# Norm, gate and weight-splitting arithmetic moved from GpSimd to VectorE in a two-block transformer kernel

## The chip, the cores and the metric

One core of one Trainium2 chip runs the whole program. The metric is device microseconds of one execution. The kernel before took 3540.33 us (median of 3 runs, 3538.97 to 3543.59). The engines are TensorE (matmul; PE in the profile, its weight loads PEld), VectorE (DVE), ScalarE (ACT), GpSimd (POOL) and SyncE (SP, which here only issues DMAs). Each engine works through its own queue in order.

## The reference, cut to what matters

The input x is 512 tokens of 1024 features, in float32. The first block repeats twice:

```
x = layer_norm(ALPHA * x + 0.5 * swiglu(x, ffn_w_in[i, 0], ffn_w_out[i, 0]), ln_g[i, 0], ln_b[i, 0])
mix = token_mix(x, ...)      # stick-breaking attention, gated delta rule, short convolution
x = layer_norm(ALPHA * x + mix, ln_g[i, 1], ln_b[i, 1])
x = layer_norm(ALPHA * x + 0.5 * swiglu(x, ffn_w_in[i, 1], ffn_w_out[i, 1]), ln_g[i, 2], ln_b[i, 2])
ple = jax.nn.sigmoid(x @ ple_w_gate[i] + ple_b_gate[i]) * (p[i] @ ple_w_proj[i])
x = layer_norm(ALPHA * x + ple, ln_g[i, 3], ln_b[i, 3])
```

The second block has one layer of dilated window attention and one of grouped attention, each with attention over 256 memory tokens, and an RMS norm ahead of the projections.

## The kernel before

Features lie on the partitions, as 8 tiles of 128 (`KD`), tokens on the free axis; `HALF` are the two halves of 256 tokens, `ALL` all 512. Nearly every float32 operand of a matmul is split in two parts of type float32r: the upper part is a copy in that type, the lower part is the value minus the upper part. A product is three matmuls: lower times upper, upper times lower, upper times upper.

**Weights** go through `Kern.weight` (L145 to L156): a DMA into `wst` (2 buffers), ScalarE's copy into `whi` (L153; 5 buffers), and a subtraction into `wlo` (L154; 5 buffers), by VectorE, or by the engine that the caller names. A `wst` buffer is free for the next load once the subtraction has read it. Where no engine is named and `K.fence` is set, the subtraction is put behind the instruction in `K.fence` on VectorE. `K.fence` is set once, by `row_rsqrt` in `RMS.scale_time` for the second half of the tokens at the end of the second `ple`: it is the last step of that norm's scale. The callers that name GpSimd: `ffn` for its first 4 tile pairs (in the first ffn of all only for one tile), all 34 units of `mixer` in each of the two layers, `ple` for its gate units (the last four of the second ple excepted), `mem_kv` of layer 0 inside the second ple (8 units) and `q_mem` of layer 0 (4 units).

**Layer norm** is the class `LN`. `add` (L267) runs after each output tile f: VectorE adds it to x (L271). At f = 0 the mean over that tile is taken through a matmul with `mean_r`, ScalarE copies it to `c` (`ln_c`, L282), and c is subtracted from all 8 tiles of x: from tile 0 by VectorE (L283), from the other seven by GpSimd (L285). For the other tiles ScalarE makes the square (L290), VectorE adds the tile to the running sum `ln_s` (L296), and the square is added to `ln_q`: by GpSimd for f = 1 to 5 (L299), by VectorE for f = 6 and 7 (L301, L303). `begin` sums `ln_s` and `ln_q` over partitions on TensorE (`ln_st`, L315), then runs a chain of small VectorE instructions on 128x2 (L319 to L323, the inverse root in L231 to L239), spreads mean and scale over the partitions on TensorE (`ln_M`, `ln_B`, L253) and subtracts the mean (L332). `end` multiplies by the scale (L343), lets ScalarE apply gain and bias (L345), copies pairs of tiles into `xh` (VectorE, L352) and makes `xl` (GpSimd, L353). `xh` and `xl` are what the next stage's matmuls read.

At the end of a stage the first half of the tokens is normed while TensorE still works on the second half, and the next stage starts on the first half while the second is normed.

**RMS norm** ahead of the second block: `RMS.write_time` splits 8 tiles for each half; every third subtraction from tile 1 on is GpSimd's (L1307).

The order on TensorE in `mixer` is written out by `weave`; elsewhere, and on the other engines, the tile framework's planner places the instructions by a timeline of its own when the program is built.

GpSimd also has work that stays: x restored from xh + xl at the end of the mixer (L592), two products in the mixer (L784, L940), rope (L1185, L1186), the softmax scale in layer A (L1379) and `RMS.add` (L1327).

Of the kernel before, what the change touches and what calls it, by code (L numbers as in the profile page):

```python
# [10 lines left out]
F = mybir.dt.float32  # L11
# [9 lines left out]
D = 1024  # L21
KD = D // 128
# [235 lines left out]
class LN:  # L258
# [7 lines left out]
    def add(self, f, ps, tk, scale):  # L266

        K, nc = self.K, self.K.nc
        y = self.y[:, f, tk]
        n = tk.stop - tk.start  # L270
        add = nc.vector.scalar_tensor_tensor(y, ps, scale, y, op0=OP.mult, op1=OP.add)  # L271
        if f == 0:
            if self.c is None:
                self.c = K.t2(name="ln_c")
                self.s = K.t2(name="ln_s")
                self.q = K.t2(name="ln_q")
            r = K.t2((128, n), FR, name="ln_r")
            nc.scalar.copy(r, y)
            p = K.mps((128, n), name="ln_p")
            nc.tensor.matmul(p, lhsT=K.mean_r, rhs=r, start=True, stop=True)  # L280
            c = self.c[:, tk]
            nc.scalar.copy(c, p)  # L282
            nc.vector.tensor_sub(y, y, c)  # L283
            for k in range(1, KD):
                nc.gpsimd.tensor_sub(self.y[:, k, tk], self.y[:, k, tk], c)  # L285
            nc.vector.tensor_copy(self.s[:, tk], y)
            nc.scalar.activation(self.q[:, tk], y, AF.Square)
            return
        sq = K.t2((128, n), name="ln_sq")
        square = nc.scalar.activation(sq, y, AF.Square)  # L290
        if f == KD - 1:
            self.lead = add, square
            if tk.start:
                self.last = sq
                return
        nc.vector.tensor_add(self.s[:, tk], self.s[:, tk], y)  # L296
        q = self.q[:, tk]
        if f < KD - 2:
            nc.gpsimd.tensor_add(q, q, sq)  # L299
        elif f == KD - 2:  # L300
            nc.vector.scalar_tensor_tensor(q, q, self.eps * D / 128, sq, op0=OP.add, op1=OP.add)  # L301
        else:
            nc.vector.tensor_add(q, q, sq)  # L303
# [31 lines left out]
    def end(self, tk, xh=None, xl=None, lead=True):  # L335

        K, nc = self.K, self.K.nc
        n = tk.stop - tk.start
        B = self.B.pop(tk.start)
        for k0 in range(0, KD, 2):  # L340
            ks = slice(k0, k0 + 2)
            y = self.y[:, ks, tk]
            mul = nc.vector.tensor_mul(y, y, B.unsqueeze(1).to_broadcast([128, 2, n]))  # L343
            for k in (k0, k0 + 1):
                act = nc.scalar.activation(self.y[:, k, tk], self.y[:, k, tk], AF.Identity, scale=self.g[:, k:k + 1],  # L345
                                           bias=self.b[:, k:k + 1])
                if lead and tk.start == 0 and k == 2:
                    K.behind([act], self.lead[1])
            if lead and tk.start == 0 and k0 == 2:
                K.behind([mul], self.lead[0])  # L350
            if xh is not None:
                nc.vector.tensor_copy(xh[:, ks, tk], y)  # L352
                nc.gpsimd.tensor_sub(xl[:, ks, tk], y, xh[:, ks, tk].bitcast(F))  # L353


def ffn(K, l, j, x, xh, xl, ln, aside=None, load=None):

    nc = K.nc
    w_in, w_out = K.i["ffn_w_in"], K.i["ffn_w_out"]
    hh, hl = [], []  # L360

    def unit(f, u):
        wh, wl = K.weight(w_in[l, j, 2 * f + u], D, nc.gpsimd if (f < 4 if load is None else f == 0 and u) else None)
        return wh.rearrange("p (k c) -> p k c", k=KD), wl.rearrange("p (k c) -> p k c", k=KD)

    def parts(W):
        return [(W[0][:, k], W[1][:, k]) for k in range(KD)]

    def moving(tk):
        return [(xh[:, k, tk], xl[:, k, tk]) for k in range(KD)]  # L370

    def swish(f, ps, tk):
        s = K.t2((128, tk.stop - tk.start), name="silu")
        K.looked.append(nc.scalar.activation(s, ps[0], AF.Silu))  # L374
        nc.vector.tensor_mul(s, s, ps[1])  # L375
        K.split(hh[f][:, tk], hl[f][:, tk], s)

    for f in range(NF):
        hh.append(K.t2(dt=FR, name="hh"))
        hl.append(K.t2(dt=FR, name="hl"))  # L380
    if load:

        first, W = 1, []
        for k in range(0, KD, 2):
            if k < 4:
                W.append(parts(unit(0, k // 2)))
            load(k)
        ps = [K.acc(name="pgu") for _ in range(2)]
        K.mm3_side([(ps[u], W[u], moving(ALL)) for u in range(2)])
        swish(0, ps, ALL)  # L390
    else:
        first = 2
        Ws = [[unit(f, 0), unit(f, 1)] for f in range(first)]
        for tk in HALF:
            ps = [[K.acc((128, 256), name="pgu") for _ in range(2)] for _ in range(first)]
            K.mm3_side([(ps[f][u], parts(Ws[f][u]), moving(tk)) for f in range(first) for u in range(2)])
            for f in range(first):
                swish(f, ps[f], tk)
        Ws = None
    for f in range(first, NF):  # L400
        W = [unit(f, 0), unit(f, 1)]
        ps = []
        for u in range(2):
            ps.append(K.acc(name="pgu"))
            K.mm3(ps[u], list(zip(parts(W[u]), moving(ALL))))
        swish(f, ps, ALL)
        if aside and f == NF // 2:
            K.masks()
            aside()

    def out_tile(f, W, tk):
        p = K.acc((128, tk.stop - tk.start), name="pfo")
        K.mm3(p, [((W[k // 8][0][:, k % 8], W[k // 8][1][:, k % 8]), (hh[k][:, tk], hl[k][:, tk])) for k in range(NF)])
        ln.add(f, p, tk, 0.5 / ALPHA)

    def out_units(f):
        W = []
        for k0 in range(0, NF, 8):
            n = min(8, NF - k0)
            a, b = K.weight(w_out[l, j, f, :, k0 * 128:(k0 + n) * 128], n * 128)  # L420
            W.append((a.rearrange("p (k c) -> p k c", k=n), b.rearrange("p (k c) -> p k c", k=n)))
        return W

    for f in range(KD - 1):
        out_tile(f, out_units(f), ALL)
    W = out_units(KD - 1)
    out_tile(KD - 1, W, HALF[0])
    ln.begin(HALF[0])
    out_tile(KD - 1, W, HALF[1])
    ln.end(HALF[0], xh, xl)  # L430
    ln.begin(HALF[1])
    ln.end(HALF[1], xh, xl)
# [40 lines left out]
def mixer(K, l, xh, xl, ln):  # L473

    nc, mm, tp = K.nc, K.mm, K.turn
# [15 lines left out]
    dt_b = cload([128, 4], ci["gdn_dt_bias"][l], "gdt")  # L491

    def unit(src):
        wh, wl = K.weight(src, D, nc.gpsimd)
        return wh.rearrange("p (k c) -> p k c", k=KD), wl.rearrange("p (k c) -> p k c", k=KD)

    def b3(col, n=128):
# [517 lines left out]
def ple(K, l, x, xh, xl, ln, rms=None, aside=None):  # L1015

    nc = K.nc
# [17 lines left out]
    for f in range(KD):  # L1035
        p = K.acc(name="ppp")
        K.mm3(p, [((Wp[f // 4][0][:, f % 4, k], Wp[f // 4][1][:, f % 4, k]), (ph[k], pl[k])) for k in range(2)])
        c = K.t2(name="pp")
# [1 line left out]
        pp.append(c)  # L1040

    def unit(f, spare=False):
        return K.unit(K.i["ple_w_gate"][l, f], None if spare else nc.gpsimd, spare)

    def some(fs, W, tk):

# [216 lines left out]
class RMS:  # L1263
# [36 lines left out]
    def write_time(self, tk):  # L1300
        K, nc = self.K, self.K.nc
        i = slice(tk.start // 4, tk.stop // 4)
        for k in range(KD):
            hv = self.h[k].rearrange("p (i c) -> p i c", c=4)
            xh, xl = by_time(self.xh[:, k])[:, i], by_time(self.xl[:, k])[:, i]
            nc.scalar.copy(xh, hv)
            (nc.gpsimd if k % 3 == 1 else nc.vector).tensor_sub(xl, hv, xh.bitcast(F))  # L1307

    def add(self, f, ps, tk):

# [203 lines left out]
def drive(first, second=(), rate=1.0):  # L1514

    live = [[0.0, n, iter(gen), 1.0 / r] for n, (gen, r) in enumerate(((first, 1.0), (second, rate)))]
    while live:
        s = min(live, key=lambda a: a[:2])
        try:
            next(s[2])  # L1520
            s[0] += s[3]
        except StopIteration:
            live.remove(s)
# [176 lines left out]
def program(tc, ins, outs):  # L1700
    with ExitStack() as ctx:
        K = Kern(ctx, tc, ins, outs)
        nc = K.nc
        xh = K.ph.tile([128, KD, S], FR, name="xh")
# [5 lines left out]
        with tc.tile_pool(name="px", bufs=1) as px:  # L1710
# [5 lines left out]
            with K.region(g=49):  # L1716
# [12 lines left out]
                parts = []  # L1729
# [4 lines left out]
                def memory(stage):  # L1734
                    if stage == 0:
                        R = K.t2((128, 256), name="mem_r")
                        nc.sync.dma_start(out=R, in_=memd[:, 2048:])
                        parts.extend(mem_parts(K, 0, R, [K.t2((128, 2, 256), FR, name="mem_p") for _ in range(8)]))
                    else:
                        drive(mem_kv(K, 0, *parts, mk, mv, nc.gpsimd, (stage - 1,)))  # L1740
                ple(K, DEPTH - 1, x, xh, xl, LN(K, x, *load_ln(K, DEPTH - 1, 3), eps), RMS(K, lambda f: x[:, f], xh, xl, g),
                    memory)
                for j in range(2):
# [178 lines left out]
```

## Time and profile before

| | |
|---|---|
| median of 3 runs | 3540.33 us (3538.97 to 3543.59) |
| the profiled execution | 3544.78 us |
| its span, first to last instruction | 3543.0 us |
| TensorE busy | 3410.4 us (96%) |
| VectorE busy | 1946.4 us (55%) |
| ScalarE busy | 1245.0 us (35%) |
| GpSimd busy | 723.7 us (20%) |
| mean granted TensorE clock | 0.975 of full speed |

Busy time is the time in which an engine had an instruction in work, whether it moved forward or stood. The granted clock is TensorE's: 1.0 is 2.4 GHz, 0.5 is 1.2 GHz; a figure between them over a stretch is the mean of the two. A wait's releaser is the instruction whose end let the waiting one start.

The stages in the trace, by time of start: ffn of layer 0 (15 us), mixer (about 380), second ffn (747), ple (1123), ffn of layer 1 (1216), mixer (1587), ffn (1955), ple with the memory projections (2331), and from about 2474 the second block's layers A and B.

### The profile page before, as it was taken

The page shows a single profiled execution, that of the slowest core. Times are in us where ns is not written, and L with a number is a line of the kernel's source. Part 1 is how long each engine was busy: PE and PEld are TensorE (multiplying, and loading weights), DVE is VectorE, ACT ScalarE, POOL GpSimd, SP SyncE. Part 2 cuts the span into 40 slices and gives each one's busy share as a digit, 9 for nine tenths or more (in the row PEclk, how much of TensorE's full clock was granted, in tenths as well). Part 3 has the DMA queues.
Part 4 walks back from the last instruction along what each step waited for, and adds up shares of the span by engine and source line. Part 5 has one row for each costly group of instructions (what it writes and reads, how often), then busy time and mean ns, then how long its engine had stood idle before and what let it go on. Part 6 is the DMA issues. An engine that isn't in the chain of part 4 may idle for free. (4 is left out here: it accounts for less than half of the span.)

```text
span 3543.0 us, 46065 instructions
## 1 busy us (share of the span) xinstructions
PE 3410.4 (96%) x17964; PEld 2900.1 (82%) x17964; DVE 1946.4 (55%) x4167; ACT 1245.0 (35%) x2104; POOL 723.7 (20%) x560
## 2 busy tenths in 40 slices
PE   8999999999999799999999999987999999999998
PEld 7888987788887788888978888876888888887777
DVE  3333665563334733346665533367867767649665
ACT  3322435332223332224353322244333333334332
POOL 0002412450012500123135200234122212111100
PEclk9999999999999899999999999997999999999999
DMA  4323211123232132232011222333222222243112
GB/s 154 109 87 98 85 36 49 37 84 101 95 92 87 48 107 98 87 93 84 34 36 61 84 100 87 98 97 122 86 85 71 69 87 73 75 133 115 54 47 79
DMA packets 91657, 294.40 MB, mean 83 GB/s; under 512 B 14256, under 2 KB 16944, under 8 KB 91312
## 3 DMA queue, kind: packets, MB, share of 16 engines
q1 hardware_dynamic: 91440, 291.47, 25.4%
q8 instruction: 141, 2.31, 0.3%
q14 instruction: 76, 0.62, 0.1%
HBM read 283.96 MB, written 7.47 MB: 82 GB/s over the span
## 5 line engine op out<-in xcount | busy, mean ns | idle before, releaser
L154 DVE TENSOR_TENSOR wlo<-wst,whi 128x1024 fp32r<-128x1024 f32 (+1 forms) x403 | 479.4, 1190 | 726.5 <-ACT whi L153 722.5
L153 ACT CAST whi<-wst 128x1024 fp32r<-128x1024 f32 (+1 forms) x520 | 530.3, 1022 | 881.1 <-issue 305.3
L188 PE MATMUL pgu<-xh,wlo 128*128 128x512 f32 (+1 forms) x1504 | 569.0, 379 | 0.2 <-ACT silu L374 0.2
L188 PE MATMUL pgu<-xl,whi 128*128 128x512 f32 (+1 forms) x1504 | 564.7, 378 | 0.0
L154 POOL TENSOR_TENSOR wlo<-wst,whi 128x1024 fp32r<-128x1024 f32 x117 | 282.0, 2416 | 577.0 <-ACT whi L153 566.7
L188 PE MATMUL pgu<-xh,whi 128*128 128x512 f32 (+1 forms) x1504 | 385.4, 379 | 12.3 <-ACT xh L176 9.1
L188 PEld LDWEIGHTS pgu<-xh,whi 128*128 128x128 f32 x1504 | 287.3, 191 | 63.8 <-ACT xh L176 9.1
L188 PEld LDWEIGHTS pgu<-xh,wlo 128*128 128x128 f32 x1504 | 287.6, 191 | 51.8 <-ACT silu L374 0.6
L188 PEld LDWEIGHTS pgu<-xl,whi 128*128 128x128 f32 x1504 | 285.0, 191 | 51.9 <-DVE xl L177 0.8
L1157 PE MATMUL p_in<-whi,xl 128*128 128x512 f32 (+1 forms) x800 | 305.1, 383 | 5.8 <-DVE xl L1307 4.5
L1157 PE MATMUL p_in<-wlo,xh 128*128 128x512 f32 (+1 forms) x800 | 305.8, 383 | 0.0
L1157 PE MATMUL p_in<-whi,xh 128*128 128x512 f32 (+1 forms) x800 | 305.2, 382 | 0.0
L285 POOL TENSOR_TENSOR x<-x,ln_c 128x256 f32<-128x256 f32 (+1 forms) x84 | 95.9, 1174 | 970.5 <-ACT ln_c L282 970.5
L188 PE MATMUL pfo<-hl,whi 128*128 128x512 f32 (+1 forms) x792 | 282.7, 366 | 0.0
L188 PE MATMUL pfo<-hh,wlo 128*128 128x512 f32 (+1 forms) x792 | 282.3, 365 | 0.0
L375 DVE TENSOR_TENSOR silu<-silu,pgu 128x512 f32<-128x512 f32 (+1 forms) x94 | 61.4, 653 | 225.1 <-PE pgu L188 190.9
L188 PE MATMUL pmx<-xl,whi 128*128 128x512 f32 (+1 forms) x480 | 180.3, 379 | 0.0
L1157 PEld LDWEIGHTS p_in<-whi,xl 128*128 128x128 f32 x800 | 151.6, 189 | 33.9 <-DVE xl L1307 4.6
L188 PE MATMUL pmx<-xh,wlo 128*128 128x512 f32 (+1 forms) x480 | 178.7, 373 | 0.0
L1157 PEld LDWEIGHTS p_in<-wlo,xh 128*128 128x128 f32 x800 | 151.7, 190 | 27.7 <-issue 2.6
L1157 PEld LDWEIGHTS p_in<-whi,xh 128*128 128x128 f32 x800 | 151.5, 189 | 27.6 <-issue 2.4
L188 PEld LDWEIGHTS pfo<-hh,wlo 128*128 128x128 f32 x792 | 149.4, 189 | 24.2
(376 smaller groups left out, 6468.7 us busy)
## 6 DMA issues: line engine op xcount, KB each, us to landing
wst<-in_ffn_w_in SPq DMA_DIRECT2D x176, 512.0 KB, 3.4
wst<-in_ffn_w_out SPq DMA_DIRECT2D x64, 512.0 KB, 3.5
wst<-in_wa_qk SPq DMA_DIRECT2D x48, 512.0 KB, 3.3
wst<-in_ffn_w_out SPq DMA_DIRECT2D x32, 384.0 KB, 3.1
wst<-in_mix_w_qkv SPq DMA_DIRECT2D x24, 512.0 KB, 3.5
wst<-in_wa_v SPq DMA_DIRECT2D x24, 512.0 KB, 3.3
wst<-in_w_gate SPq DMA_DIRECT2D x24, 512.0 KB, 3.2
wst<-in_w_out SPq DMA_DIRECT2D x32, 384.0 KB, 3.1
```

Source lines behind the costliest of these rows:

```text
L153: nc.scalar.copy(hi, st)
L154: sub = (eng or nc.vector).tensor_sub(lo, st, hi.bitcast(F))
L188: return self.nc.tensor.matmul(out, lhsT=lhsT, rhs=rhs, start=start, stop=stop)
L285: nc.gpsimd.tensor_sub(self.y[:, k, tk], self.y[:, k, tk], c)
L375: nc.vector.tensor_mul(s, s, ps[1])
L1157: K.nc.tensor.matmul(out, lhsT=w, rhs=x, start=(j == 0), stop=(j == n - 1))
```

## The change

The subtraction of c from tiles 1 to 7 (L285) and the adding of squares (L299) go to VectorE, as do all weight subtractions named above, but for one tile of the very first ffn and the four units of `q_mem`. In `LN.end` ScalarE makes `xh` in place of VectorE, and VectorE makes `xl` in place of GpSimd. In `RMS.write_time` VectorE makes all of `xl`. The eight units of `mem_kv` inside the second ple name no engine any more, so that those that come after `K.fence` is set (the four of its last call) stand behind it.

```diff
             for k in range(1, KD):
-                nc.gpsimd.tensor_sub(self.y[:, k, tk], self.y[:, k, tk], c)
+                nc.vector.tensor_sub(self.y[:, k, tk], self.y[:, k, tk], c)
...
         q = self.q[:, tk]
-        if f < KD - 2:
-            nc.gpsimd.tensor_add(q, q, sq)
-        elif f == KD - 2:
+        if f == KD - 2:
             nc.vector.scalar_tensor_tensor(q, q, self.eps * D / 128, sq, op0=OP.add, op1=OP.add)
         else:
             nc.vector.tensor_add(q, q, sq)
...
             if xh is not None:
-                nc.vector.tensor_copy(xh[:, ks, tk], y)
-                nc.gpsimd.tensor_sub(xl[:, ks, tk], y, xh[:, ks, tk].bitcast(F))
+                nc.scalar.copy(xh[:, ks, tk], y)
+                nc.vector.tensor_sub(xl[:, ks, tk], y, xh[:, ks, tk].bitcast(F))
...
     def unit(f, u):
-        wh, wl = K.weight(w_in[l, j, 2 * f + u], D, nc.gpsimd if (f < 4 if load is None else f == 0 and u) else None)
+        wh, wl = K.weight(w_in[l, j, 2 * f + u], D, nc.gpsimd if load and f == 0 and u else None)
...
     def unit(src):
-        wh, wl = K.weight(src, D, nc.gpsimd)
+        wh, wl = K.weight(src, D)
...
     def unit(f, spare=False):
-        return K.unit(K.i["ple_w_gate"][l, f], None if spare else nc.gpsimd, spare)
+        return K.unit(K.i["ple_w_gate"][l, f], None, spare)
...
             nc.scalar.copy(xh, hv)
-            (nc.gpsimd if k % 3 == 1 else nc.vector).tensor_sub(xl, hv, xh.bitcast(F))
+            nc.vector.tensor_sub(xl, hv, xh.bitcast(F))
...
-                        drive(mem_kv(K, 0, *parts, mk, mv, nc.gpsimd, (stage - 1,)))
+                        drive(mem_kv(K, 0, *parts, mk, mv, None, (stage - 1,)))
```

## Rows read from the trace of the kernel before

**Rows 1.** The page's part 1: busy us of each engine, share of the span, instructions.

```profile
PE 3410.4 (96%) x17964; PEld 2900.1 (82%) x17964; DVE 1946.4 (55%) x4167; ACT 1245.0 (35%) x2104; POOL 723.7 (20%) x560
```

**Rows 2.** Busy us by stretch: bounds, length, PE, PEld, DVE, ACT, POOL; PEclk, DMA.

```profile
366.00:676.00 310.00, 300.24 (x1863) 257.14 (x1862) 200.57 (x409) 141.96 (x274) 97.40 (x54) 0.99 0.17 52
676.00:760.00 84.00, 73.28 (x511) 71.09 (x510) 56.55 (x102) 25.35 (x48) 47.95 (x39) 0.86 0.19 64
1112.00:1240.00 128.00, 101.41 (x696) 96.16 (x695) 94.28 (x166) 51.30 (x97) 73.79 (x53) 0.85 0.18 58
1578.00:1885.00 307.00, 298.48 (x1828) 255.44 (x1829) 199.62 (x405) 141.83 (x273) 97.40 (x54) 0.98 0.16 51
1885.00:1968.00 83.00, 73.91 (x506) 71.84 (x505) 55.98 (x101) 24.64 (x47) 47.77 (x38) 0.84 0.20 64
2320.00:2440.00 120.00, 96.29 (x614) 88.82 (x613) 93.01 (x192) 57.13 (x109) 61.18 (x45) 0.88 0.25 85
2440.00:2480.00 40.00, 26.96 (x114) 23.20 (x115) 27.73 (x70) 19.23 (x41) 13.24 (x9) 0.63 0.58 190
```

**Rows 3.** Waits of TensorE: who waited for whom, total us, times, longest us.

```profile
PE ln_B L253 <- DVE bc_l L250: 16.8, 6, 5.1
PE pg L188 <- ACT sig L1055: 16.7, 6, 4.8
PE ppp L188 <- DVE p_l L177: 8.7, 2, 4.3
```

**Rows 4.** Timeline, end of layer 0's mixer, VectorE: start, us, instruction.

```profile
682.75 2.38 DVE L177 TENSOR_TENSOR mxl<-sc_o,mxh 128x512 fp32r<-128x512 f32 x1 [0.68 <-ACT mxh L176]
728.78 0.16 DVE L319 TENSOR_SCALAR ln_m<-ln_st 128x2 f32<-128x2 f32 x1 [0.74 <-PE ln_st L315]
736.62 2.24 DVE L250 TENSOR_TENSOR bc_l<-ln_r,bc_h 128x2 fp32r<-128x2 f32 x1
```

**Rows 5.** Timeline of VectorE, the same chain with GpSimd idle (end of ffn).

```profile
1110.57 0.16 DVE L319 TENSOR_SCALAR ln_m<-ln_st 128x2 f32<-128x2 f32 x1 [2.88 <-PE ln_st L315]
...
1111.16 0.17 DVE L231 TENSOR_SCALAR rs_y<-ln_v 128x2 int32<-128x2 int32 x1
...
1113.32 0.16 DVE L250 TENSOR_TENSOR bc_l<-ln_r,bc_h 128x2 fp32r<-128x2 f32 x1
```

**Rows 6.** Timeline of VectorE and GpSimd in layer 0's ple.

```profile
1205.24 2.29 DVE L231 TENSOR_SCALAR rs_y<-ln_v 128x2 int32<-128x2 int32 x1
...
1205.16 2.34 POOL L154 TENSOR_TENSOR wlo<-wst,whi 128x1024 fp32r<-128x1024 f32 x1 [0.17 <-ACT whi L153]
```

**Rows 7.** Groups by line and shape: count | busy us, mean ns | idle before.

```profile
L154 POOL TENSOR_TENSOR wlo<-wst,whi 128x1024 fp32r<-128x1024 f32 x117 | 282.0, 2416 | 577.0 <-ACT whi L153 566.7 <-DVE xl L177 9.9
L353 POOL TENSOR_TENSOR xl<-x,xh 128x512 fp32r<-128x512 f32 x56 | 77.3, 1400 | 53.7 <-DVE xh L352 33.9 <-DVE ln_m L321 11.1 <-DVE rs_b L237 4.0
...
L154 DVE TENSOR_TENSOR wlo<-wst,whi 128x1024 fp32r<-128x1024 f32 x339 | 417.8, 1233 | 492.6 <-ACT whi L153 488.8 <-PE p_in L1157 0.9 <-PE att_T L183 0.9
L271 DVE SCALAR_TENSOR_TENSOR x<-pfo,x 128x512 f32<-128x512 f32 x28 | 19.2, 684 | 2.7 <-PE pfo L188 2.7
L271 DVE SCALAR_TENSOR_TENSOR x<-pmo,x 128x256 f32<-128x256 f32 x32 | 13.4, 419 | 33.1 <-PE pmo L188 33.1
...
L176 ACT CAST hh<-silu 128x512 fp32r<-128x512 f32 x82 | 50.3, 614 | 11.0 <-DVE silu L375 11.0
```

**Rows 8.** Waits of VectorE, the longest in total.

```profile
DVE wlo L154 <- ACT whi L153: 722.5, 317, 9.7
```

**Rows 9.** Timeline of TensorE around the last norm of the second ple.

```profile
2449.21 0.62 PE L1157 MATMUL p_mkv<-whi,mem_p 128*128 128x512 f32 x2
2449.66 0.39 PE L1157 MATMUL p_mkv<-wlo,mem_p 128*128 128x512 f32 x1
2449.89 0.62 PE L1157 MATMUL p_mkv<-whi,mem_p 128*128 128x512 f32 x2
...
2468.24 0.45 PE L253 MATMUL rms_B<-ident_r,bc_l 128*128 128x128 f32 x1 [7.54 <-DVE bc_l L250]
...
2473.77 0.80 PE L1157 MATMUL p_in<-whi,xl 128*128 128x512 f32 x1 [4.45 <-DVE xl L1307]
```

## Prediction

> **What bounds the kernel now.** I read the page's busy line first, then the stretches with TensorE's clock, then what TensorE waited for, then the timelines of the places so found. TensorE is busy 96% of the span [rows 1]: it is the bound, and a change on other engines can only give back what TensorE loses in waits or at a low clock. The seven stretches of [rows 2] are the stage ends and the two mixers; outside them lie the four ffns, and from 2480 us on the change touches nothing but an order. In these rows length less TensorE's busy time is 9.8 + 10.7 + 26.6 + 8.5 + 9.1 + 23.7 + 13.0 = 101 us of waits. The clock adds to it: one minus PEclk, times the busy time, is 3.0 + 10.3 + 15.2 + 6.0 + 11.8 + 11.6 + 10.0 = 68 us. So about 169 us, in 1072 us of the span, can be had at most.
>
> The waits are for VectorE, directly or through ScalarE: ln_B waits for bc_l, the last link of the norm's chain, pg for a sigmoid that stands behind VectorE's steps on the tile before it, ppp for a VectorE subtraction [rows 3]. And VectorE is slow there for one reason that the reader should see. The root's first step on 128x2 takes 0.17 us when GpSimd is idle [rows 5]. In the ple it takes 2.29 us: it starts 0.08 us after GpSimd's wlo and ends with it, at 1207.5 us [rows 6]. The chain from ln_m to bc_l takes 1113.48 - 1110.57 = 2.9 us alone [rows 5] and 738.86 - 728.78 = 10.1 us beside GpSimd [rows 4]; its last step is held 2.24 us. A split of 128x512 takes 2.38 us there [rows 4], where such an operation takes about 0.68 [rows 7]. An instruction of VectorE that overlaps one of GpSimd thus stands until that ends, and all behind it stand too.
>
> The Trainium skill, SBUF — State Buffer, section "SBUF: two separate sides", has a rule for this: VectorE and GpSimd share one pair of ports, taken for a whole instruction. By that rule the trace agrees (2.29 us beside a 2.34 us wlo).
>
> **The change part by part.**
>
> *Weight subtractions.* GpSimd has 117 at 2.42 us [rows 7]; 5 stay (one in the first ffn, four of q_mem), 112 move: 24 in three ffns, 68 in the mixers, 12 in the ples, 8 in mem_kv. On VectorE one is 1.23 us [rows 7], so 138 us come to it. In the ffns neither costs anything: no row of [rows 2] or [rows 3] has a TensorE wait there, and VectorE already makes most weights of those stages so; without that cover each would cost 1.2 us. In a chain a hold of up to 2.4 us becomes one instruction of 1.2 us at most. Their DMAs stay on SP's queue; a wst buffer comes free 1.2 us earlier.
>
> *Running sums and means.* L285 is 28 of 128x512 (7 in each of four ffns) and 56 of 128x256; L299 is 20 and 40. At 0.68 and 0.42 us [rows 7] that is 48 x 0.68 + 96 x 0.42 = 73 us for VectorE. In the ffns' output phase TensorE never waits. In a mixer or ple half, seven subtractions (2.9 us) come right after tile 0; tile 1 needs only its own, so 0.4 us of them lies on the path.
>
> *xh and xl.* 56 pairs: VectorE's copy becomes its subtraction, one for one, and ScalarE gets 56 x 0.61 = 34 us [rows 7]. GpSimd's 1.40 us per xl [rows 7] becomes 0.68. Ahead of the first matmul of a stage the way is then gain and bias, copy 0.61, subtraction 0.68, in place of copy 0.42 to 0.68 (VectorE's 128x256 and 128x512 rows [rows 7] as ends) and 1.40: 0.5 to 0.8 us less, and the norm's second chain isn't held by the four xl. ScalarE's four copies (2.5 us) stand ahead of whatever it does next; in the ple that is p_h.
>
> *The six of L1307* add under 4 us to VectorE.
>
> So VectorE takes on some 138 + 73 + 4 = 215 us and GpSimd leaves it alone. Now the path, place by place; each is "waits now, less what I expect".
>
> 1. Mixer's end into ffn (10.7 and 9.1 us). The lower part of sc_o is held 1.7 us [rows 4], and another before it alike: 3. The chain is held 10.1 - 2.9 = 7.2 us; three subtractions and two adds now made beside it by GpSimd may fall into it, 3 x 1.23 + 2 x 0.42 = 4.5, so it gains 2.7 to 7.2 against a wait of 3.5 us: 3. The first xh and xl: 1. Together 7 per layer, 14.
> 2. ffn into ple (part of the 26.6 and 23.7). ppp's wait of 4.3 us [rows 3] stands behind held roots; ScalarE's 2.5 us of copies come ahead of p_h: 2. ln_M's wait in front of it: 1. Together 6.
> 3. First ple. VectorE is busy 94 of 128 us [rows 2] with holds like that of [rows 6] on nearly each tile. Each costs the next tile's sigmoid up to 2.3 - 1.2 = 1.1 us, and eight GpSimd subtractions fall in it: 9.
> 4. Second ple up to 2440 us: the same with mem_kv's subtractions beside it: 5.
> 5. Mixers and their starts (9.8 and 8.5 us): holds like those of [rows 6] become 1.2 us; two or three of 1.1 us each per layer lie on a path: 5. GpSimd's restoring of x stays and still holds VectorE.
> 6. 2440 to 2480 us, **the added wait**. The last four mem_kv subtractions now stand behind the fence. Three of their products take 2449.89 - 2449.21 = 0.68 us [rows 9], the 48 of them 10.9 us, at half clock 21.8. They ran while VectorE was in the norm's chain. Now they come after it, into the wait of 4.45 us [rows 9]. Behind the waiting subtraction on VectorE stand rms_h and xl of the last half, and TensorE for them; q_mem's loads wait on SP's queue for the two wst buffers, and GpSimd splits each at 2.42 us. Against that TensorE and ScalarE are free for the norm, whose scale was waited for 7.54 us [rows 9]. Bounds: a gain of 12 us (7.54 + 4.45) to a loss of 17 (21.8 - 4.45); I take 0, as the waits (12) and the products at full clock (11) are of one size.
>
> Waits: 14 + 6 + 9 + 5 + 5 + 0 = 39 us of 101. The clock fell where TensorE waited (PEclk 0.99 where 3% is idle, 0.63 where a third is [rows 2]); the same share of 68 us is 26, and since it comes back in steps and the last stretch (10.0) keeps its waits, I take 20. VectorE now stands in order behind ScalarE's whi, 722.5 / 317 = 2.3 us on average where it already does so [rows 8]; bounds 0 to 37 us (rival 2), of which I take 10. Sum: 39 + 20 - 10 = 49 us. The profiled execution took 3544.8 us, its span 3543.0; it lies 4.5 us above the median of the runs. 3544.8 - 49 = 3495.8, and against the median **3491 us**.
>
> **The rivals.**
>
> 1. *No net change* (3534 to 3547 us). VectorE's queue takes over the holds: 39 + 20 is eaten by its waits for whi and by the planner's new order. For it: VectorE's busy time hardly falls, 215 us come and the holds that go are of about that size. Against it: what comes is 1.2 us each, in places chosen at build time, where the holds struck a chain at random.
> 2. *Slower, the mixer's queue.* The mixers take 68 subtractions into a VectorE that is busy 201 of 310 us [rows 2] and feeds TensorE link by link. With a wait w for whi ahead of each, VectorE stands 68 x (w + 1.23) us where today it is held some 50 (an estimate: one hold of 2.3 us [rows 6] for every third unit). Today the mixers lose 18.3 us in waits, of which I put 10 down to those 50, a rate of 0.2. The gain elsewhere, 59 less the mixers' 5, is 54. It decides from 0.2 x (68 x (w + 1.23) - 50) = 54, w = 3.5 us, against 2.3 measured in the ffns; at 5 us TensorE loses 75 us and the time is 3561. At 2.3 it is 38, the 37 above.
> 3. *VectorE is full.* It is busy 57 of 84 and 94 of 128 us at the stage ends [rows 2]; if its long instructions were its own and not GpSimd's doing, some 60 of the 215 us would fall there and the time would be 3600 us. Against it: 0.17 against 2.29 us for one instruction. The Trainium skill, Perfetto Trace Analysis, section "Optimizing Scalar/DVE Operations", says that work of a saturated VectorE may be given to ScalarE or GpSimd, and in the same place that the latter shares a read port with it; the first half speaks against this change, the trace bears out the second.
> 4. *More than I take.* If TensorE's waits end sooner and the clock hardly falls, two thirds of the 169 us less 13.0 and 10.0 come back: 0.67 x 146 = 98, 3442 us.
>
> **How the numbers follow.** Forecast (3455 to 3530) 0.70; rival 4 0.10; rival 1 0.10; rival 2 0.07; rival 3 0.03. A difference under 0.2%, 7 us, can't be told from no change. Faster is 0.70 + 0.10 = 0.80, same 0.10, slower 0.07 + 0.03 = 0.10. The range is 3450 to 3540: below it lies part of rival 4, above it part of rival 1 and rivals 2 and 3; its ends also take the fence's bounds (12 and 15 us) and the 37 us of the queue.
>
> **What would show it.** VectorE's 128x2 steps at 0.16 to 0.17 us everywhere in the first block, but for the places where GpSimd restores x; the ln_B wait down from 16.8 us to under 8; PEclk above 0.9 in 676 to 760 us; xl after xh by 0.7 us. The fence shows as matmuls of p_mkv after the last rms_B. I am wrong if VectorE stands for whi with tiles queued behind it (rival 2: its waits for whi in the mixers over 3.5 us each), or if the half-clock stretches keep their length with shorter waits, which would leave 39 - 10 = 29 us, 3511.

## The result, and the profile after

The changed kernel takes 3498.1 us (median; 3497.0 to 3499.6) where the kernel before takes 3539.7 us beside it: a ratio of 0.9881 (0.9864 to 0.9898), 41.5 us less. The profiled execution took 3497.5 us, with a span of 3495.8 us, 47.2 us less than the profiled one of before.

The page's part 1 after the change (busy us of each engine, share, instructions); it answers to [rows 1]:

```profile
PE 3383.5 (97%) x17964; PEld 2876.7 (82%) x17964; DVE 1957.3 (56%) x4429; ACT 1273.2 (36%) x2160; POOL 210.7 (6%) x242
```

GpSimd lost 513 us of work, ScalarE got 28, and VectorE got 262 instructions and yet only 11 us of busy time. The moved work fills time in which VectorE's instructions had been standing (held time, below: 194 us before, 8.5 us after).

The stretches, as in [rows 2], bounded by the start of the same matmuls, with an eighth one right behind them (bounds, length, PE, PEld, DVE, ACT, POOL, PEclk, DMA share, GB/s):

```profile
365.00:671.00 306.00, 298.10 (x1860) 255.75 (x1859) 205.74 (x436) 145.69 (x282) 21.66 (x19) 0.99 0.16 51
671.00:745.00 74.00, 67.47 (x516) 65.79 (x515) 54.24 (x134) 27.07 (x51) 0.00 (x0) 0.95 0.22 72
1097.00:1214.00 117.00, 99.29 (x694) 95.02 (x694) 85.00 (x204) 61.04 (x115) 0.00 (x0) 0.87 0.20 67
1552.00:1857.00 305.00, 297.09 (x1833) 254.71 (x1833) 205.56 (x433) 146.16 (x282) 21.66 (x19) 0.98 0.16 51
1857.00:1929.00 72.00, 65.46 (x505) 63.95 (x504) 52.77 (x133) 25.42 (x50) 0.00 (x0) 0.95 0.23 74
2282.00:2388.00 106.00, 90.08 (x607) 83.96 (x605) 83.81 (x219) 57.17 (x112) 0.00 (x0) 0.90 0.23 76
2388.00:2425.00 37.00, 28.81 (x119) 24.50 (x119) 28.28 (x81) 20.94 (x43) 3.46 (x2) 0.68 0.55 192
2425.00:2455.00 30.00, 20.04 (x87) 16.21 (x86) 15.04 (x46) 9.51 (x13) 6.11 (x3) 0.86 0.54 188
```

The seven stretches are 55 us shorter (1017 for 1072). Worked out as ahead of the change, length less TensorE's busy time, their waits went from 101.4 to 70.7 us, and one minus PEclk times the busy time went from 67.8 to 46.7 us. The eighth row gives part of that back: a new wait of 10.0 us, and 2.8 us of clock (the kernel before has neither in its 30 us from 2480 us on). The rest, 5 us, lies in the ffns and in the late part.

Waits of TensorE after the change (who waited for whom, total us, times, longest us); the first and the fourth answer to [rows 3], and the wait of ppp for VectorE is no longer among the long ones:

```profile
PE pg L188 <- ACT sig L1053: 13.0, 6, 5.1
PE nh_t L183 <- issue: 10.0, 1, 10.0
PE ln_M L253 <- DVE bc_l L250: 9.5, 2, 4.9
...
PE ln_B L253 <- DVE bc_l L250: 4.6, 1, 4.6
```

The norm's second chain at the end of layer 0's mixer, VectorE, which answers to [rows 4]:

```profile
733.60 0.15 DVE L317 TENSOR_SCALAR ln_m<-ln_st 128x2 f32<-128x2 f32 x1
733.67 0.68 DVE L351 TENSOR_TENSOR xl<-x,xh 128x512 fp32r<-128x512 f32 x1
...
735.20 0.17 DVE L231 TENSOR_SCALAR rs_y<-ln_v 128x2 int32<-128x2 int32 x1
...
738.48 0.16 DVE L250 TENSOR_TENSOR bc_l<-ln_r,bc_h 128x2 fp32r<-128x2 f32 x1
```

From ln_m to the end of bc_l it takes 738.64 - 733.60 = 5.0 us, with VectorE's four xl in between, in place of 10.1. No link of it is longer than 0.17 us. In the whole first block 45 of VectorE's 319 instructions that write 128x2 took over 0.5 us before; after, none does.

The groups of the moved operations (count | busy us, mean ns | idle before), which answer to [rows 7]:

```profile
L154 DVE TENSOR_TENSOR wlo<-wst,whi 128x1024 fp32r<-128x1024 f32 x451 | 553.2, 1227 | 552.0 <-ACT whi L153 548.7 <-PE p_in L1155 0.9 <-PE p_gate L1155 0.4
...
L351 DVE TENSOR_TENSOR xl<-x,xh 128x512 fp32r<-128x512 f32 x56 | 38.0, 687 | 19.8 <-ACT xh L350 19.7
...
L350 ACT CAST xh<-x 128x512 fp32r<-128x512 f32 x56 | 32.7, 612 | 0.0
```

### The profile page after: what moved, and what is told of

Its sections match the earlier page's. It is cut to its first block, busy times and chain, and to the rows that moved or that the text cites. A ratio compares the mean times of both kernels' runs of the same rounds, so it can differ in the third digit from the quotient of the medians.

```text
span 3495.8 us, 45870 instructions
## 1 busy us (share of the span) xinstructions
PE 3383.5 (97%) x17964; PEld 2876.7 (82%) x17964; DVE 1957.3 (56%) x4429; ACT 1273.2 (36%) x2160; POOL 210.7 (6%) x242
## 5 line engine op out<-in xcount | busy, mean ns | idle before, releaser
L154 DVE TENSOR_TENSOR wlo<-wst,whi 128x1024 fp32r<-128x1024 f32 (+1 forms) x515 | 614.8, 1195 | 766.5 <-ACT whi L153 763.0
L188 PEld LDWEIGHTS pfo<-hl,whi 128*128 128x128 f32 x792 | 149.3, 189 | 24.2
L188 PE MATMUL pfo<-hh,whi 128*128 128x512 f32 (+1 forms) x792 | 167.4, 366 | 0.0
```

The costliest lines, as they stand in the source:

```text
L154: sub = (eng or nc.vector).tensor_sub(lo, st, hi.bitcast(F))
L188: return self.nc.tensor.matmul(out, lhsT=lhsT, rhs=rhs, start=start, stop=stop)
```

## What was to be told apart

**Theory H** (holding): VectorE's instructions stand while a GpSimd instruction runs, and the change pays because the chains on VectorE no longer stand. **Theory Q** (late results): GpSimd's own results, wlo at 2.4 us and xl at 1.4 us, came late to TensorE. Beside these, the new wait of 10 us had to be explained, and why the waits fell by less than was forecast.

The trace of the kernel before already speaks on Q. Of some 129 us of TensorE's waits, these two are put down to a GpSimd instruction, 0.9 us in all:

```profile
PE rr_st L1121 <- POOL rms_q L1327: 0.5, 1, 0.5
PE ln_st L315 <- POOL wlo L154: 0.4, 1, 0.4
```

VectorE waits 4.1 us for a GpSimd ln_q and ScalarE 4.8 us for a GpSimd wlo. So late results show little in the waits; the planner may still have put TensorE's work in another order because of them.

For the runs below, "held time" is worked out from the trace: over VectorE's instructions in the first 2500 us that overlap one of GpSimd, the duration less the 10th percentile of the same line and shape. It is 194 us in the kernel before and 8.5 us after. "Idle" is TensorE's idle time over the whole span; "clock" is half of TensorE's busy time in the stretches at the lower level.

## Holding against late results

### GpSimd works for nobody

On top of the kernel after; `ghost` is true for the units of the ffn, the mixer and the ple gates that the change moved. The buffer `junk` that nobody reads needs room in SBUF, so the ring `g` has 48 buffers in place of 49.

```diff
         sub = (eng or nc.vector).tensor_sub(lo, st, hi.bitcast(F))
+        if ghost:
+            nc.gpsimd.tensor_sub(self.junk[:, :n], hi.bitcast(F), hi.bitcast(F))
...
-            with K.region(g=49):
+            with K.region(g=48):
```

> The kernel after, and for each weight unit of the ffn, the mixer and the two ple gates whose subtraction the change moved, GpSimd makes a subtraction of the same size (whi minus whi) into a buffer that nobody reads; the ring g has 48 buffers in place of 49, to make room for it. No wait of TensorE, VectorE or ScalarE for GpSimd is added, but for the reuse of whi. Theory H (VectorE's instructions stand while a GpSimd instruction runs): steps of 128x2 at 1.2 to 2.3 us again at the stage ends, and the time goes back most of the way, 3520 to 3540 us. Theory Q (in the kernel before the moved results themselves came late, at 2.4 us for each wlo): as the kernel with 48 buffers alone, 3498 us within 5.

> The kernel after with 48 buffers in place of 49 in the ring g, and nothing else: the yardstick for the run with the unread subtractions. Both theories: 3498 us within 3, as no wait of TensorE in the kernel after goes back to that ring.

Measured: 48 buffers alone 3497.6 us, ratio 0.9874 (0.9859 to 0.9889), the same as the kernel after. With the unread subtractions 3562.3 us, ratio 1.0058 (1.0043 to 1.0073): 65 us more, and 21 us slower than the kernel before. Theory Q has no place for that. Nor has the planner's order: in order of start, the instructions of TensorE (17964), of VectorE (4429) and of ScalarE (2160) are the same by operation, tiles and shape, one for one, in these two runs, and no wait of TensorE, VectorE or ScalarE is put down to an unread subtraction. Theory H is borne out in its direction and was too low in size: VectorE now has the moved work and stands as well (held time 121 us, on 2067.7 us of busy time); that this is why it is slower than the kernel before is argued, not shown. The stretches of the first mixer, its end and the ple, the group of the unread work, and one place in the mixer, of the run with it:

```profile
365.00:685.00 320.00, 303.89 (x1867) 260.63 (x1865) 230.91 (x437) 146.40 (x282) 87.64 (x46) 0.97 0.16 49
685.00:770.00 85.00, 72.28 (x510) 70.27 (x509) 66.12 (x133) 26.78 (x51) 23.25 (x10) 0.86 0.20 63
1122.00:1249.00 127.00, 100.21 (x697) 95.61 (x696) 102.07 (x206) 61.42 (x115) 32.88 (x14) 0.85 0.20 61
```

```profile
L156 POOL TENSOR_TENSOR junk<-whi 128x1024 bf16<-128x1024 f32 x104 | 253.3, 2436 | 1996.2 <-ACT whi L153 1995.0
```

```profile
466.31 1.89 POOL L156 TENSOR_TENSOR junk<-whi 128x1024 bf16<-128x1024 f32 x1 [5.96 <-ACT whi L153]
466.77 1.46 DVE L237 TENSOR_TENSOR rs_a<-rs_n 128x8 f32<-128x8 f32 x1
468.15 1.28 DVE L759 TENSOR_TENSOR U<-N,masks 128x512 f32<-128x512 f32 x2
...
470.57 1.28 DVE L760 TENSOR_TENSOR U<-ident,U 128x512 f32<-128x512 f32 x2
471.39 1.09 PE L185 MATMUL pT<-ident,U 128*128 128x128 f32 x4 [6.08 <-DVE U L760]
```

The mixer's row has 16.1 us of waits where the kernel after has 7.9, and the mixer's end 12.7 for 6.5. The small step rs_a starts inside the unread subtraction, ends with it, 0.03 us behind, and all of U stands behind it; TensorE waits 6.08 us for U, where it waits 2.69 us in the kernel after.

### The weights alone

```diff
-        wh, wl = K.weight(w_in[l, j, 2 * f + u], D, nc.gpsimd if (f < 4 if load is None else f == 0 and u) else None)
+        wh, wl = K.weight(w_in[l, j, 2 * f + u], D, nc.gpsimd if load and f == 0 and u else None)
...
-        wh, wl = K.weight(src, D, nc.gpsimd)
+        wh, wl = K.weight(src, D)
...
-        return K.unit(K.i["ple_w_gate"][l, f], None if spare else nc.gpsimd, spare)
+        return K.unit(K.i["ple_w_gate"][l, f], None, spare)
```

> The kernel before, with only the weight subtractions of the ffn, the mixer and the ple gates on VectorE; norms, the xh/xl split and the memory's k and v stay as before. H: VectorE stands less at the stage ends, and most of the gain is there, 3505 to 3520 us. Q (the late xl is the larger part): 3530 to 3540 us, since xl is still GpSimd's.

Measured: 3506.6 us, ratio 0.9894 (0.9880 to 0.9909): 37.2 us of gain. Idle falls from 132.6 to 114.0 us, clock from 65.5 to 46.0, held time from 194 to 101. As H expected.

### The norms alone, the split of x alone

```diff
# the norms, in the kernel before
-                nc.gpsimd.tensor_sub(self.y[:, k, tk], self.y[:, k, tk], c)
+                nc.vector.tensor_sub(self.y[:, k, tk], self.y[:, k, tk], c)
...
-            nc.gpsimd.tensor_add(q, q, sq)
+            nc.vector.tensor_add(q, q, sq)
```

```diff
# the split, in the kernel before
-                nc.vector.tensor_copy(xh[:, ks, tk], y)
-                nc.gpsimd.tensor_sub(xl[:, ks, tk], y, xh[:, ks, tk].bitcast(F))
+                nc.scalar.copy(xh[:, ks, tk], y)
+                nc.vector.tensor_sub(xl[:, ks, tk], y, xh[:, ks, tk].bitcast(F))
```

> The kernel before with only the running sums and means of the norms (L285 and L299) on VectorE. H, as the run with the weights alone gave 37 of the 41 us and little is left for the other parts: the weights' GpSimd instructions still hold VectorE, and of the shorter ones that go (56 of 128x256 and 28 of 128x512 in L285, 60 in L299) few lie beside a chain, 3530 to 3538 us where before is 3541. Rival (the parts pay alike, by the time that they take off GpSimd): some 10 us less than before for this one, 3528 to 3533 us.

> The kernel before with only the split of x changed: ScalarE makes xh, VectorE xl, all else as before. If the late xl of 1.4 us was on TensorE's path: 3515 to 3530 us. If only the holding by the weights counts: 3536 to 3543 us, as pmx and pgu then still wait for xh, which comes behind four L343 on ScalarE.

Measured: the norms 3529.9 us, ratio 0.9962 (0.9948 to 0.9977), 13.3 us; the split 3526.2 us, ratio 0.9953 (0.9938 to 0.9968), 16.9 us. The run of the norms lies where both expectations meet and decides nothing between them. The split is worth far more than the 0 to 7 us that followed from "only the weights count": that fell, and the time lies in the range given for a late xl. TensorE's waits for the last link in the two runs, the norms' first:

```profile
PE ln_B L253 <- DVE bc_l L250: 8.1, 6, 2.6
```

```profile
PE ln_B L253 <- DVE bc_l L250: 17.4, 6, 5.1
```

The norms' move halves the wait of [rows 3]; the split leaves it, and takes its gain elsewhere (the wait of ppp for p_l, 8.7 us in [rows 3], is down to two waits of 0.5 and 0.4 us in layer 0). The three parts alone give 37.2 + 13.3 + 16.9 = 67.4 us, more than all together (41.5, or 55.9 without the fence's price, below). A wait at the end of a chain with two holds can be won back by ending either, and only once; that this makes the difference, and not the work that comes to VectorE, is not shown.

### The split where nothing else holds VectorE

Three kernels on top of the one with the fence lifted (3487.9 us, below): the split as in the kernel before; both halves on VectorE; and the latter with an unread subtraction on GpSimd.

```diff
# as before
-                nc.scalar.copy(xh[:, ks, tk], y)
-                nc.vector.tensor_sub(xl[:, ks, tk], y, xh[:, ks, tk].bitcast(F))
+                nc.vector.tensor_copy(xh[:, ks, tk], y)
+                nc.gpsimd.tensor_sub(xl[:, ks, tk], y, xh[:, ks, tk].bitcast(F))
```

```diff
# both on VectorE, and (last line, with g=48) the unread one
-                nc.scalar.copy(xh[:, ks, tk], y)
+                nc.vector.tensor_copy(xh[:, ks, tk], y)
...
+                nc.gpsimd.tensor_sub(K.junk[:, :, :n], y, xh[:, ks, tk].bitcast(F))
```

> The kernel after with the fence lifted for the memory's k and v (3488 us), and the split as in the kernel before: VectorE makes xh, GpSimd xl. If the change of the split pays where the weights no longer hold VectorE: 3493 to 3500 us, with 128x2 steps at 1.4 us in the second chain. If it pays nothing: 3486 to 3490 us.

> The same, but VectorE makes both xh and xl; ScalarE makes neither and GpSimd has no xl. If ScalarE's copies behind its four L343 are what keeps the wait of 2.0 us ahead of pgu and pmx: these waits fall to 1.5 us or less, and the time is 3480 to 3486 us. If VectorE's queue is the tighter one at the stage ends (56 copies of 0.68 us more on it): 3490 to 3496 us.

> The kernel in which VectorE makes both xh and xl and the fence is lifted (3491 us), and for each xl GpSimd makes the same subtraction once more into a buffer that nobody reads; the ring g has 48 buffers. TensorE's xl is VectorE's and isn't late. If it is the holding of VectorE by which a GpSimd xl costs the 15 us between the two last runs: 3502 to 3508 us, with 128x2 steps at 1.1 to 1.4 us in the second chain. If it is that GpSimd's xl itself comes late: 3491 us within 4. In between if both: some 3495 to 3500 us.

Measured: the old split 3505.4 us, ratio 0.9896 (0.9881 to 0.9911), 17.5 us more than 3487.9, and more than either expectation. Both halves on VectorE 3490.7 us, ratio 0.9854 (0.9838 to 0.9870): not to be told from ScalarE making xh. So what pays in the split is that xl leaves GpSimd; who makes xh doesn't matter. The waits for xh of the mixer's and the ffn's first products, pmx and pgu, did not fall either (2.8 and 2.7 us for 2.1 and 2.0), so ScalarE's copies behind L343 were not what kept them. With the unread subtraction 3522.7 us, ratio 0.9952 (0.9936 to 0.9968): 32 us more, though TensorE reads nothing of GpSimd's xl there and the instructions of TensorE, VectorE and ScalarE again start in the same order in both. GpSimd, then VectorE, at the end of layer 0's mixer in that run:

```profile
738.46 7.45 POOL L352 TENSOR_TENSOR junk<-x,xh 128x512 f32<-128x512 f32 x4 [92.11 <-DVE ln_m L317]
...
739.29 1.28 DVE L319 TENSOR_TENSOR ln_m<-ln_m 128x2 f32<-128x2 f32 x1
...
741.57 1.16 DVE L250 TENSOR_TENSOR bc_l<-ln_m,bc_h 128x2 fp32r<-128x2 f32 x1
...
742.98 1.77 DVE L351 TENSOR_TENSOR xl<-x,xh 128x512 fp32r<-128x512 f32 x1
```

Holding is thus enough to explain the 15 us between the two runs before it. That it overshoots fits VectorE's own xl being held too (1257 ns in the mean of 56, for 687 without the unread work), so that it does come late: TensorE's pmx and pgu wait 7.8 us for it. In the run with the old split no wait of TensorE is put down to a GpSimd xl; if a late xl costs there, it is through the planner's order, which differs between these two runs (TensorE's in some 170 of 17964 places). How the 15 us divide between the chain and a late xl stays open.

## The new wait at q_mem

```diff
# once
-                        drive(mem_kv(K, 0, *parts, mk, mv, None, (stage - 1,)))
+                        drive(mem_kv(K, 0, *parts, mk, mv, nc.gpsimd, (stage - 1,)))
```

```diff
# and once
+                        held, K.fence = K.fence, None
                         drive(mem_kv(K, 0, *parts, mk, mv, None, (stage - 1,)))
+                        K.fence = held
```

> The kernel after, with the memory's k and v weights alone back on GpSimd, so that their unit is no longer held behind the fence of the last ple. If the fence is what makes the 10 us wait of TensorE at q_mem (2443.10 in the kernel after): that wait goes, about 3488 us, less some 3 to 5 us if GpSimd then holds the chain at the end of that ple, so 3488 to 3493. If the wait has another cause: 3498 us.

> The kernel after, with the fence lifted while the memory's k and v are made, so that the subtraction of their weights is VectorE's and is not held behind the norm. If the fence makes the 10 us wait at q_mem: 3486 to 3490 us. If not: 3498 us. If a subtraction in VectorE's queue ahead of the norm's chain costs as much as GpSimd holding it did: 3492 to 3498 us, with the wait moved to the root's chain at 2400.

Measured: on GpSimd 3488.9 us, ratio 0.9848 (0.9833 to 0.9862); with the fence lifted 3487.9 us, ratio 0.9846 (0.9830 to 0.9863). Both are some 10 us faster than the kernel after (some 13 to 14 by the gain on the kernel before beside each), and the wait is gone in both: it was the fence. Where it bites is seen on SP's queue, then on ScalarE, VectorE and TensorE, in the kernel after:

```profile
2407.56 1.47 SPq L150 DMA_DIRECT2D wst<-in_w_mem_kv  x2
...
2414.58 0.33 SPq L150 DMA_DIRECT2D wst<-in_w_qm  x1
...
2430.08 0.33 SPq L150 DMA_DIRECT2D wst<-in_wa_qk  x1
```

```profile
2441.20 1.05 ACT L153 CAST whi<-wst 128x1024 fp32r<-128x1024 f32 x1 [5.65 <-DMA wst<-in_wa_qk]
...
2443.41 1.56 ACT L1165 ACTIVATE nh_y<-p_in 128x512 f32<-128x512 f32 x3
...
2447.05 0.16 DVE L237 SCALAR_TENSOR_TENSOR rs_b<-rs_a,nh_v 128x4 f32<-128x4 f32 x1
2447.88 1.23 DVE L154 TENSOR_TENSOR wlo<-wst,whi 128x1024 fp32r<-128x1024 f32 x1 [0.66 <-ACT whi L153]
2449.02 0.15 DVE L239 SCALAR_TENSOR_TENSOR rs_n<-rs_b,rs_y 128x4 f32<-128x4 f32 x1
2450.27 1.23 DVE L154 TENSOR_TENSOR wlo<-wst,whi 128x1024 fp32r<-128x1024 f32 x1 [1.10 <-ACT whi L153]
2451.41 0.15 DVE L235 TENSOR_TENSOR rs_a<-rs_n 128x4 f32<-128x4 f32 x1
...
2453.06 1.20 PE L183 MATMUL nh_t<-ident,nh_y 128*128 128x128 f32 x4 [9.96 <-issue]
```

and on SP's queue with the fence lifted:

```profile
2377.52 10.48 SPq L150 DMA_DIRECT2D wst<-in_w_qm  x4
2390.94 0.62 SPq L150 DMA_DIRECT2D wst<-in_wa_qk  x1
```

The subtractions of mem_kv hold the two wst buffers until the norm's scale is made; so the loads of w_qm start at 2414.58 in place of 2377.52 us and those of wa_qk at 2430.08 in place of 2390.94. Then ScalarE stands 5.65 us for a load of wa_qk, and behind that copy stand the squares (nh_y) with which the norm of q_mem's first three units begins: they start together at 2443.41, where with the fence lifted each starts by itself, the first at 2423.53. Two subtractions for wa_qk stand in VectorE's queue between the links of that norm (rs_b, rs_n, rs_a), each waiting for its whi, 4.2 us with their waits, and TensorE waits for nh_t.

## A theory that fell: VectorE's queue at the stage ends

In the kernel after a subtraction of 1.22 us runs ahead of the last L271 (375.21 us), TensorE's wait for ln_st there rose from 0.37 to 1.45 us, and another stands between links at 1107. Two kernels with the fence lifted for mem_kv put the next stage's subtractions behind the last addition, or behind the broadcast of the mean:

```diff
                 self.last = sq
+                K.fence = add
```

```diff
-        K.bcast(M.rearrange("p (t c) -> p t c", c=128), m)
+        K.fence = K.bcast(M.rearrange("p (t c) -> p t c", c=128), m)
```

> The kernel after with the fence lifted for the memory's k and v (3488 us when it ran), and with every weight subtraction of a next stage put behind the last addition of a stage (the last L271 of its second half) in VectorE's queue. If a subtraction ahead of that addition is what lengthened the wait ahead of ln_st from 0.37 to 1.45 us: the wait is 0.3 to 0.5 us again at four stage ends, 4 us in all and some 2 us of clock behind it, 3481 to 3485 us. If something else ends that wait: 3488 us.

> The same, but with the subtractions behind the broadcast of the mean (the last L250 of ln_m) of a stage's second half. If VectorE's queue at the stage ends is what took back the expected gain: the wait ahead of ln_M (4.65 us at 1104) falls by the 1.2 us of the subtraction between its links, the wait ahead of ln_st to 0.4 us, and the time is 3476 to 3484 us. The rival: the first units of a next stage then come late, pmx and pgu wait for wlo at 380 and 734, and the time is 3490 us or more.

Measured: 3503.4 us, ratio 0.9896 (0.9879 to 0.9912), and 3501.6 us, ratio 0.9888 (0.9873 to 0.9902): 15.5 and 13.7 us slower than without the order. The wait ahead of ln_st did go in both, and that ahead of ln_M fell to 1.9 us in the second. But others came. TensorE's waits, first of the second kernel, then of the one without the order:

```profile
PE pg L188 <- ACT sig L1053: 19.3, 7, 7.2
PE ln_M L253 <- DVE bc_l L250: 12.7, 7, 2.1
...
PE ppp L188 <- ACT p_h L176: 4.6, 4, 2.4
```

```profile
PE pg L188 <- ACT sig L1053: 13.3, 6, 5.1
...
PE ln_M L253 <- DVE bc_l L250: 8.6, 2, 4.6
```

Idle is 109.9 us for 103.5, clock 40.8 for 32.9 (the profiled execution without the order lies 6 us under its median, so part of that is scatter). In the first kernel ppp waits 11.5 us for p_l and p_h. A subtraction that is held back is late later; the planner's order was the better one. The rival's time came for the second kernel, its reason (pmx and pgu waiting for wlo) only in small part: 0.55 and 0.41 us there. In the first kernel pgu waits 1.40 us for wlo at 731.5.

## Why the prediction was right, and where its sum was off

The forecast was 3491 us, 49 us less; measured are 3498.1 and 41.5. The time lies in the range, and the mechanism is the one named: the unread work shows it apart from everything else. The kernels before and after also differ in the planner's order (TensorE's in some 300 of 17964 places); what that gives or takes no run separates. All signs named are there: 128x2 steps at 0.15 to 0.17 us in the first block (8 of 319 at 0.21); the ln_B wait 4.6 us (under 8); PEclk 0.95 in the mixer's end (above 0.9); xl in 0.68 us; p_mkv's products from 2407.6 us, right behind the last rms_B.

Rival 3 (VectorE is full) is out: 262 more instructions made it 11 us busier. Rival 2 is out in the mixers. VectorE's waits there, in 365 to 672 us of the kernel after:

```profile
DVE wlo L154 <- ACT whi L153: 16.0, 10, 2.7
```

That is 1.6 us each for 10 of the 34, against the 3.5 us from which it would have decided. Its mechanism exists all the same: it is part of the wait of 10 us at q_mem.

The terms, place by place (forecast, then the rows of before less those of after):

- Mixer's end: 14; 4.19 + 2.55 = 6.7. The chain gave its 3.5 us (ln_B's wait is gone). The split of sc_o was held once, not twice (2.03 to 0.95 us), the first xh came no sooner (pgu waits 2.04 for 1.79, in layer 1 2.05 for 0.71), and ln_st waits 1.58 for 0.55, as the last running sum now stands behind VectorE's four L330. The step that failed is "another before it alike" and the 1 us for xh.
- Into the first ple and the ple: 3 + 9; 8.9. Into the second and that one: 3 + 5; 7.8. In sum near the forecast, but ln_M's wait on the way in, forecast to fall by 1 us, rose from 3.1 to 4.7 and from 3.4 to 4.9: a weight subtraction and xl of VectorE stand between its links. ppp's waits there fell by more than forecast, from 4.9 to 1.4 and to nothing.
- Mixers and their starts: 5; 2.5. The step that failed is the rule itself: "an instruction of VectorE that overlaps one of GpSimd stands until that ends" is too wide (last section). At the mixers' starts the instructions beside the chain that read PSUM were never held.
- The fence: 0 within -17 to +12; 13.0 - 8.2 - 10.0 = -5.1. That the waits of the seventh stretch fell from 13.0 to 8.2 us is only in small part the fence's doing: with it lifted they are 9.9 (1.1 for rms_st, 5.0 for rms_B, 3.8 for xl). The products did fill the waits for rms_B and xl (3.0 us left for 8.8), but where they had stood, nh_t of the memory's keys now waits 5.2 us. So the fence itself saves 1.7 us there and costs 10.0 behind. What was left out is what stood behind the products: the loads on SP's queue were named and not followed to the next stage. With its clock this is the 10 us that both runs on it gave back.
- Waits in all: 39; 20.8. Clock: 20; 67.8 - 46.7 - 2.8 = 18.3, nearly as forecast.
- VectorE's queue: 10 us off. Outside q_mem its marks are ln_st at six stage ends, which waits 9.0 us in all for 2.2, and ln_M into the two ples, 9.5 for 6.5. These lie in the rows above and are not a term beside them; the attempts to take them away lost time.

The rows thus give 20.8 + 18.3 = 39.1 of the 47.2 us; 5 lie outside the stretches, the rest is in their rounded bounds and clocks. Without the fence the gain is 55.9 us, more than forecast. So the mechanism was right, and that the sum came so near was in part luck: the waits less the queue were put at 29 us and are 20.8, the mixers' ends gave half of their term, the fence took 8 us where nothing was put, and 5 us came in the ffns and the late part, where nothing was put either.

## What to carry to other kernels

Where an instruction takes ten times its length beside another engine's, give that engine work that nobody reads: one run separates "it holds others" from "its result is late", if all other instructions keep their order. When a step is put behind a fence, follow the load buffers that it keeps to the loads queued behind them and into the next stage; here the price was paid there. Causes taken away singly can give more in sum than together: do not add such gains up.

## What the runs showed of the hardware

Not every VectorE instruction is held. GpSimd, then VectorE, at the end of the first ffn in the kernel before:

```profile
374.49 4.71 POOL L154 TENSOR_TENSOR wlo<-wst,whi 128x1024 fp32r<-128x1024 f32 x2 [10.23 <-ACT whi L153]
374.07 2.48 DVE L332 TENSOR_TENSOR x<-x,ln_M 128x512 f32<-128x512 f32 x4 [0.69 <-PE ln_M L253]
376.47 0.42 DVE L271 SCALAR_TENSOR_TENSOR x<-pfo,x 128x256 f32<-128x256 f32 x1
376.80 2.47 DVE L343 TENSOR_TENSOR x<-x,ln_B 128x512 f32<-128x512 f32 x4
```

All nine run at their plain length (0.68 and 0.42 us each), eight of them started inside the two GpSimd subtractions. Each has one operand that TensorE has just written (ln_M, pfo, ln_B, in PSUM). In the kernel before up to 2480 us, of the VectorE instructions that start inside one of GpSimd that outlasts their plain length, none of L332 (15) and L343 (12) was held, and each of L250 (13), L235 (12), L239 (11) and of the copies L352 (16), which read SBUF alone, was held to its end. L271 was held in the ple, where it reads sig from SBUF (2.4 us at 1183 and at 2406), and not in the ffn and the mixer, where it reads PSUM. In layer A, beside GpSimd's softmax scale (L1379), only 13 of 57 such steps of L235 and L239 were held; what sets these apart stays open.

The Trainium skill, SBUF — State Buffer, section "SBUF: two separate sides", has this limit: the port pair is contested by VectorE instructions with two SBUF inputs or in a two-port mode, and whoever starts first keeps it. Up to 2480 us the rows agree on the first. One place agrees on the second: in the run with unread subtractions one of these took 2.95 us (375.57 to 378.52) behind a subtraction of VectorE that had started 0.02 us ahead of it, for 1.89 us when alone. The prediction took the first half of the rule and left out the limit, though the row above stood in the trace of before.
